# Weight parts at eight offsets in larger buffers, and backward columns in every other tile of the second up product

## The chip, the cores and the metric

The kernel runs on one core of a Trainium2 chip. The metric is device microseconds of one execution, from the median of several timed runs. Engines are named as in the profile: PE (matmuls; PEld are its weight loads), DVE (elementwise), ACT (activations and casts), POOL and SP (here mostly issuers of DMAs).

## The reference

One layer of a streaming encoder on 512 tokens of width 1024, all in float32: a half-step SwiGLU feed-forward, a mixer of chunked attention and trailing means, a second half-step feed-forward, a final norm.

```python
x = x + 0.5 * swiglu_ffn(rmsnorm(x, ffn1_norm[l]), ffn1_w_gate[l], ffn1_w_up[l], ffn1_w_down[l])
x = x + hybrid_mixer(rmsnorm(x, mix_norm[l]), w_in[l], ...)
x = x + 0.5 * swiglu_ffn(rmsnorm(x, ffn2_norm[l]), ffn2_w_gate[l], ffn2_w_up[l], ffn2_w_down[l])
x = rmsnorm(x, final_norm[l])
...
def swiglu_ffn(x, w_gate, w_up, w_down):      # w_gate, w_up: 1024 x 2816, w_down: 2816 x 1024
    return (jax.nn.silu(x @ w_gate) * (x @ w_up)) @ w_down
```

## The kernel before

**Products of float32 from three matmuls.** Each operand is split into two parts of type float32r, `hi` (a cast by ACT) and `lo` (the rest, by DVE), in `split`, or in `high` and `low` within the up product. `mm3` multiplies hi by hi (L170), hi of the loaded operand by lo of the streamed one (L171), and lo by hi (L172). In a matmul the first argument after the output is the loaded (stationary) operand, 128 columns wide, and the next is streamed, 128, 256 or 512 columns wide; in the profile `mm<-ha,whi` is a matmul into `mm` that streams `ha` and has loaded `whi`.

**Stages.** The first up product (gate and up projections of the first feed-forward, `ffn_up` with `loaded=False`), the first down product (`Down`), the mixer, the second up product (`ffn_up` with `loaded=True`), the second down product. In an up product the weights are loaded and the normalised activations streamed; in a down product the activations (`ah`) are loaded and the weights streamed.

**Up products.** There are 22 tiles of 128 features. The first five are made plainly, with 512 columns a matmul. The other 17 (`for n in range(PLAIN, KF)`) use a Strassen-like scheme: seven products A11, S3, S2, A22, S1, A12, S4 of half size, each made by `product`: four slices times the three matmuls of `mm3`, 12 matmuls with 256 columns (`HT`), 84 a tile. Each `product` writes into half of a PSUM bank, `acc`, `up_lo` or `up_hi`, and ACT or DVE takes it from there. The loop's order on PE, DVE and ACT is written out by hand (`manual_schedule`). The streamed operands `norm.a[...]` are tiles of the h pool (`ha`), of the pool that held x (`xa`) or of the activation pool (`sa`, for S4 alone). The weight parts come in the order 22, 11, 13, 24: from the loaded blocks, or from sums that DVE makes of them.

**Where weight parts lie.** `part_tiles` gives the next pair of buffers of 1024 columns. From `Down.begin` on, `part_rooms` has four places: three times the weight pool and then the activation pool, so every fourth pair lies in the activation pool. In the loop that is the part for 13, which S3 and S1 use. In the down products `Down.weights` takes its parts from the same places, and the plain tiles do through `weights`. The mixer makes its weights in `prepare`, with tiles of its own of the same tags, and does not go through `part_tiles`.

**What sets the order elsewhere.** In the mixer a planner with costs and ranks orders the work; in the down products the framework's scheduler does. The weights come from memory through SP's queue, and POOL's queue makes sums of blocks of the down weights in memory with accumulating DMAs, paced by small `mark` copies.

Of the kernel before, what the change touches and what calls it, by code (L numbers as in the profile page):

```python
# [9 lines left out]
F32R = mybir.dt.float32r  # L10
# [6 lines left out]
P = 128  # L17
# [29 lines left out]
def layer(  # L47
# [44 lines left out]
    def name(what):  # L92
        n_tiles[0] += 1
        return f"{what}_{n_tiles[0]}"

    def temp(dtype=F32):
        return tpool.tile([P, S], dtype, tag="t", name=name("t"))

    def bank(tag="mm", bufs=4):
        return ps.tile([P, S], F32, tag=tag, name=name(tag), bufs=bufs)  # L100

    def abank():
        return bank("a", 4)
# [36 lines left out]

    part_rooms: list = [(wpool, HILO)]
    n_parts = [0]

    def part_tiles():
        pool, bufs = part_rooms[n_parts[0] % len(part_rooms)]
        n_parts[0] += 1
        return (
            pool.tile([P, 1024], F32R, tag=tag, name=name("w" + tag), bufs=bufs)
            for tag in ("hi", "lo")
        )  # L150

    def weights(src, parts=1):
        n = src.shape[-1]
        raw = raw_tile()
        hi, lo = part_tiles()
        for i in range(parts):
            part = slice(i * n // parts, (i + 1) * n // parts)
            nc.sync.dma_start(raw[:, part], src[:, part])
            split(raw[:, part], hi[:, part], lo[:, part])
        return hi, lo  # L160
# [6 lines left out]
    def mm3(acc, a, b, start, stop, further=False):  # L167

        more = dict(skip_group_check=True) if further else {}
        nc.tensor.matmul(acc, a[0], b[0], start=start, stop=False, **more)  # L170
        nc.tensor.matmul(acc, a[0], b[1], start=False, stop=False, **more)  # L171
        nc.tensor.matmul(acc, a[1], b[0], start=False, stop=stop, **more)  # L172

    def cut(pair, lo, n):
        return pair[0][:, lo : lo + n], pair[1][:, lo : lo + n]


    def residual_tiles():
        pairs = [xpool.tile([P, 2 * S], F32, tag=f"x{k}", name=name("x")) for k in range(KD // 2)]
        return [pairs[k // 2][:, k % 2 * S : (k % 2 + 1) * S] for k in range(KD)]  # L180

    x = residual_tiles()
# [208 lines left out]
    def ffn_up(norm, wA, down, loaded):  # L391
# [21 lines left out]
        for kp in range(KD // 2):  # L413
            if not loaded:
                load(2 * kp)
            w = weights(wA[kp], 1 if loaded or kp else 4)
# [7 lines left out]
            for kk in range(2):  # L424
                k = 2 * kp + kk
# [10 lines left out]
        raws, w = {}, {}  # L436

        def fetch(n):

            if n < KF:  # L440
                f = down.order[n]
                raw = raws[n] = down.pool.tile([P, 4 * S], F32, tag="raw", name=name("raw"), bufs=RAW)
                nc.sync.dma_start(raw[:, S : 3 * S], wA[2 * f])
                nc.sync.dma_start(
                    raw.rearrange("p (b c) -> p b c", c=S)[:, 0:4:3],
                    wA[2 * f + 1].rearrange("p (b c) -> p b c", c=S),
                )

        def high(n, what, src):
            hi, lo = (z[:, : src.shape[-1]] for z in part_tiles())  # L450
            nc.scalar.copy(hi, src)  # L451
            w[what] = hi, lo, src

        def low(what):
            hi, lo, src = w[what]
            nc.vector.tensor_tensor(lo, src, hi.bitcast(F32), op=ALU.subtract)  # L456
# [5 lines left out]
        def high11(n):  # L462
            if n < KF:
                high(n, (n, 11), raws[n][:, :S])

        def low11(n):
            if n < KF:
                low((n, 11))

        def sum13(n):  # L470
            if n < KF:
                z = w[n, "odd"] = new_sum()
                raw = raws[n]
                nc.vector.tensor_tensor(z, raw[:, : 2 * S], raw[:, S : 3 * S], op=ALU.add)

        def sum24(n):
            if n < KF:
                z = w[n, "even"] = new_sum()
                raw, odd = raws[n], w[n, "odd"]
                nc.vector.tensor_tensor(z[:, :S], odd[:, :S], raw[:, 2 * S : 3 * S], op=ALU.add)  # L480
                nc.vector.tensor_tensor(z[:, S:], z[:, :S], raw[:, 3 * S :], op=ALU.add)

        def high13(n):
            if n < KF:
                high(n, (n, 13), w[n, "odd"])

        def low13(n):
            if n < KF:
                low((n, 13))

        def high24(n):
            if n < KF:
                high(n, (n, 24), w[n, "even"])

        def low24(n):
            if n < KF:
                low((n, 24))

        for n, f in enumerate(down.order[2 : PLAIN - 1], 2):
            banks = []  # L500
            for j in range(2):
                wj = weights(wA[2 * f + j])
                acc = bank()
# [7 lines left out]
        n, f = PLAIN - 1, down.order[PLAIN - 1]  # L511
# [23 lines left out]
        down.open(range(G - 3, G))  # L535

        def product(acc, part, a, start):
            for k in range(4):
                mm3(
                    acc, cut(part, k * P, P), [z[k] for z in norm.a[a]],  # L540
                    start and k == 0, k == 3, not start,
                )

        def copy(dst, src, scale=1.0):
            nc.scalar.activation(dst, src, AF.Copy, scale=scale)  # L545
# [7 lines left out]
        with tc.manual_schedule(engines={E.PE, E.DVE, E.Activation}):  # L553
            last_silu = last_place = last_sums = nothing
            for n in range(PLAIN, KF):
                f = down.order[n]
                acc, up_lo, up_hi = bank()[:, :HT], bank()[:, :HT], abank()[:, :HT]
                u, z, sg = temp(), temp(), temp()
                w11, w13, w24 = (w[n, i][:2] for i in (11, 13, 24))
                product(acc, w11, A11, True)  # L560
                last_silu()
                last_place()
                high(n, (n, 22), raws[n][:, 2 * S :])
                low((n, 22))
                w22 = w[n, 22][:2]
                copy(u[:, :HT], acc)
                product(up_hi, cut(w13, S, S), S3, True)
                fetch(n + 2)
                high11(n + 1)
                low11(n + 1)  # L570
                last_sums()
                sum13(n + 1)
                copy(z[:, HT:], up_hi, -1.0)
                product(acc, cut(w24, 0, S), S2, False)
                copy(u[:, HT:], acc, -1.0)
                sum24(n + 1)
                product(up_hi, cut(w24, S, S), A22, False)
                nc.vector.tensor_tensor(u[:, HT:], up_hi, u[:, HT:], op=ALU.add)  # L578
                down.make_sums(u[:, HT:])
                product(acc, cut(w13, 0, S), S1, False)  # L580
                copy(z[:, :HT], acc)
                nc.vector.tensor_tensor(z[:, HT:], z[:, :HT], z[:, HT:], op=ALU.add)
                high13(n + 1)
                low13(n + 1)
                high24(n + 1)
                product(up_lo, cut(w22, S, S), A12, True)
                nc.scalar.activation(sg[:, HT:], z[:, HT:], AF.Silu)
                nc.vector.tensor_tensor(u[:, :HT], up_lo, u[:, :HT], op=ALU.add)
                low24(n + 1)
                product(acc, cut(w22, 0, S), S4, False)  # L590

                def last_silu(acc=acc, sg=sg):
                    nc.scalar.activation(sg[:, :HT], acc, AF.Silu, scale=-1.0)

                def last_place(f=f, u=u, sg=sg):
                    down.place(f, u, sg)

                def last_sums(f=f):
                    down.sums(f)

            last_silu()
            last_place()
            last_sums()
# [7 lines left out]
    class Down:  # L611
# [74 lines left out]
        def weights(self, i, g):  # L686

            src = self.rows(i, g)
            n = groups[g][1] * S
            raw = raw_tile()[:, :n]  # L690
            hi, lo = part_tiles()
            if tuple(src.shape[1:]) == (groups[g][1], S):
                load_now(raw.rearrange("p (k c) -> p k c", c=S), src)
                split(raw, hi[:, :n], lo[:, :n])
            else:

                load_now(raw.rearrange("p (d c) -> p d c", d=S // P), src)
                split(
                    raw.rearrange("p (d k c) -> p k d c", d=S // P, c=P),
                    *(z[:, :n].rearrange("p (k d c) -> p k d c", d=S // P, c=P) for z in (hi, lo)),  # L700
                )
            return hi, lo
# [636 lines left out]
    with tc.tile_pool(name="act2", bufs=1, reuse_waits="tile") as apool:  # L1339
        down2.begin(apool)  # L1340

        for half in range(2):
            for t in range(NT):
# [5 lines left out]
                z = temp()  # L1349
# [196 lines left out]
```

## Time and profile before

| | us |
|---|---|
| timed runs: median | 885.51 |
| timed runs: lowest, highest of 3 | 883.26, 889.71 |
| profiled execution: span | 887.8 |
| PE busy in it | 861.2 |
| DVE busy | 710.9 |
| ACT busy | 500.4 |

The span goes from the first to the last instruction of the one profiled execution; the profile gives no other time for that execution. The granted clock averages 0.987 over the span. Busy times of different engines overlap. Matmuls overlap too: one takes 282 ns (256 columns) or some 395 ns (512 columns) from its start to its modelled end, and the next starts long before, so times are read from start to start.

### The profile page before, as it was taken

The page shows a single profiled execution, that of the slowest core. Times are in us where ns is not written, and L with a number is a line of the kernel's source. Part 1 is how long each engine was busy: PE and PEld are TensorE (multiplying, and loading weights), DVE is VectorE, ACT ScalarE, POOL GpSimd, SP SyncE. Part 2 cuts the span into 40 slices and gives each one's busy share as a digit, 9 for nine tenths or more (in the row PEclk, how much of TensorE's full clock was granted, in tenths as well). Part 3 has the DMA queues.
Part 4 walks back from the last instruction along what each step waited for, and adds up shares of the span by engine and source line. Part 5 has one row for each costly group of instructions (what it writes and reads, how often), then busy time and mean ns, then how long its engine had stood idle before and what let it go on. Part 6 is the DMA issues. An engine that isn't in the chain of part 4 may idle for free.

```text
span 887.8 us, 14123 instructions
## 1 busy us (share of the span) xinstructions
PE 861.2 (97%) x5296; PEld 764.4 (86%) x5296; DVE 710.9 (80%) x1128; ACT 500.4 (56%) x852; POOL 122.3 (14%) x197
## 2 busy tenths in 40 slices
PE   9999999999799999989999999999999999899995
PEld 7889999999778887867877788889999999788885
DVE  7899889888668768686777476969889888777897
ACT  7455555555556556547757455445555555565572
POOL 0112222122300000120020000102222112300011
PEclk9999999999899999999999999999999999999998
DMA  7258879797996663222120126247868787997522
GB/s 284 69 170 232 248 202 230 201 219 177 286 274 201 203 200 121 106 83 83 72 72 25 48 95 232 95 124 220 240 218 226 202 210 194 271 344 262 212 97 95
DMA packets 71955, 158.49 MB, mean 179 GB/s; under 512 B 6080, under 2 KB 29136, under 8 KB 71504
## 3 DMA queue, kind: packets, MB, share of 16 engines
q1 hardware_dynamic: 49088, 111.45, 35.6%
q0 software_dynamic: 22656, 46.14, 24.3%
q8 instruction: 41, 0.67, 0.3%
q14 instruction: 26, 0.21, 0.1%
q10 hardware_dynamic: 144, 0.01, 0.0%
HBM read 153.38 MB, written 50.34 MB: 229 GB/s over the span
## 4 chain that ended last, share of the span: by engine, by line
PE 54%; DVE 4%; ACT 1%; DMA 1%; issue 1%; POOLq 0%; POOL 0%; ACTq 0%
PE mm L170 13%; PE mm L171 13%; PE mm L172 13%; PE a L170 3%; PE a L172 3%; PE a L171 3%; PE a L1161 1%; DMA raw<-in_wB_dram 1%; PE a L1107 1%; PE a L1149 1%; DVE t L1028 1%; DVE wlo L123 1%; PE a L1346 0%; PE a L1036 0%; ACT prob L1088 0%
## 5 line engine op out<-in xcount | busy, mean ns | idle before, releaser
L122 ACT CAST whi<-raw 128x1024 fp32r<-128x1024 f32 (+2 forms) x107 | 102.7, 968 | 80.5 <-PE mm L171 20.4
L123 DVE TENSOR_TENSOR wlo<-raw,whi 128x1024 fp32r<-128x1024 f32 (+2 forms) x107 | 119.4, 1121 | 33.6 <-ACT whi L122 32.7
L172 PE MATMUL mm<-ha,wlo 128*128 128x256 f32 x408 | 115.3, 283 | 0.0
L170 PE MATMUL mm<-ha,whi 128*128 128x256 f32 x408 | 115.2, 282 | 0.0
L171 PE MATMUL mm<-ha,whi 128*128 128x256 f32 x408 | 115.2, 282 | 0.0
L545 ACT ACTIVATE t<-mm 128x256 f32<-128x256 f32 x102 | 39.2, 384 | 118.1 <-PE mm L172 117.4
L456 DVE TENSOR_TENSOR wlo<-wsum,whi 128x1024 fp32r<-128x1024 f32 x68 | 83.0, 1221 | 14.4 <-ACT whi L451 14.4
L170 PEld LDWEIGHTS mm<-ha,whi 128*128 128x128 f32 x408 | 78.2, 192 | 0.1
L171 PEld LDWEIGHTS mm<-ha,whi 128*128 128x128 f32 x408 | 77.5, 190 | 0.1
L172 PEld LDWEIGHTS mm<-ha,wlo 128*128 128x128 f32 x408 | 77.5, 190 | 0.0
L666 POOL DMA_DIRECT2D wsum<-in_wB_dram x72 | 71.7, 1150 | 36.5 <-DMA wsum<-wsum 28.3
L170 PE MATMUL mm<-hhi,whi 128*128 128x512 f32 x192 | 75.9, 398 | 0.3 <-ACT whi L122 0.3
L171 PE MATMUL mm<-hlo,whi 128*128 128x512 f32 x192 | 75.7, 395 | 0.0
L172 PE MATMUL mm<-hhi,wlo 128*128 128x512 f32 x192 | 74.9, 392 | 0.0
L170 PE MATMUL mm<-whi,ah 128*128 128x512 f32 x176 | 69.7, 396 | 1.3 <-ACT whi L122 1.3
L664 POOL COPY mark<-t 128x1 f32<-128x1 f32 x40 | 13.3, 332 | 416.4 <-DVE t L578 237.5
L451 ACT CAST whi<-wsum 128x1024 fp32r<-128x1024 f32 x68 | 68.0, 1047 | 4.3 <-PE mm L171 4.1
L171 PE MATMUL mm<-wlo,ah 128*128 128x512 f32 x176 | 69.4, 395 | 0.8 <-DVE wlo L123 0.8
L172 PE MATMUL mm<-whi,ah 128*128 128x512 f32 x176 | 69.3, 394 | 0.0
L456 DVE TENSOR_TENSOR wlo<-raw,whi 128x512 fp32r<-128x512 f32 x68 | 62.4, 953 | 0.5 <-ACT whi L451 0.5
L123 DVE TENSOR_TENSOR ah<-acts,ah 128x512 fp32r<-128x512 f32 (+1 forms) x72 | 47.6, 667 | 17.1 <-ACT ah L122 17.1
L451 ACT CAST whi<-raw 128x512 fp32r<-128x512 f32 x68 | 56.2, 826 | 5.9 <-PE mm L171 4.4
(211 smaller groups left out, 2418.5 us busy)
## 6 DMA issues: line engine op xcount, KB each, us to landing
raw<-in_wA_dram SPq DMA_DIRECT2D x87, 512.0 KB, 5.4
wsum<-in_wB_dram POOLq DMA_DIRECT2D x60, 512.0 KB, 7.6
raw<-wsum SPq DMA_DIRECT2D x40, 512.0 KB, 4.3
raw<-in_wB_dram SPq DMA_DIRECT2D x30, 512.0 KB, 4.7
wsum<-wsum POOLq DMA_DIRECT2D x20, 512.0 KB, 4.9
x<-in_xT_dram SPq DMA_DIRECT2D x16, 256.0 KB, 7.4
raw<-in_wQK_dram SPq DMA_DIRECT2D x8, 512.0 KB, 3.6
raw<-in_wO_dram SPq DMA_DIRECT2D x8, 512.0 KB, 3.4
```

Of the source, the lines that this page charges most:

```text
L122: nc.scalar.copy(hi, src)
L123: nc.vector.tensor_tensor(lo, src, hi.bitcast(F32), op=ALU.subtract)
L170: nc.tensor.matmul(acc, a[0], b[0], start=start, stop=False, **more)
L171: nc.tensor.matmul(acc, a[0], b[1], start=False, stop=False, **more)
L172: nc.tensor.matmul(acc, a[1], b[0], start=False, stop=stop, **more)
L451: nc.scalar.copy(hi, src)
L456: nc.vector.tensor_tensor(lo, src, hi.bitcast(F32), op=ALU.subtract)
L545: nc.scalar.activation(dst, src, AF.Copy, scale=scale)
L664: nc.gpsimd.tensor_copy(mark, after[:, 0:1])
L666: nc.gpsimd.dma_start(self.rows(i, g), self.rows(self.terms[i][at], g), **(dict(accum_op=ALU.add) if at else {}),)
L1028: nc.vector.tensor_tensor(q3, q3, rs[:, t, :].unsqueeze(2).to_broadcast([P, 8, HD]), op=ALU.mult)
L1107: nc.tensor.matmul(sc[i][:, :n], qT[pair][0][a][rows, t * P : (t + 1) * P], kT[pair][0][b][rows, :n], start=a + b == 0, stop=a == 1,)
```

## The change

Parts lie in buffers of 1056 columns in place of 1024, 128 bytes more on each partition, and begin `at` columns of 4 bytes into them. `at` goes through 0, 4, ... 28 with the count of parts, that is 0, 16, ... 112 bytes, shifted by one step after each four parts; both parts of a pair have the same `at`. All other tiles keep their places modulo 128 bytes.

In the half-size tiles of the second up product (`loaded`) with even n (6, 8, ... 20, eight of the 17), `product` hands the streamed operand and the output to `mm3` with the columns reversed. Each result column lands where it did before. The names, shapes and order of the instructions on each engine are the same in both programs.

```diff
@@ part_tiles
     n_parts = [0]
+    back = [False]
 
     def part_tiles():
         pool, bufs = part_rooms[n_parts[0] % len(part_rooms)]
+        at = 4 * ((n_parts[0] + n_parts[0] // 4) % 8)
         n_parts[0] += 1
         return (
-            pool.tile([P, 1024], F32R, tag=tag, name=name("w" + tag), bufs=bufs)
+            pool.tile([P, 1024 + 32], F32R, tag=tag, name=name("w" + tag), bufs=bufs)[:, at : at + 1024]
             for tag in ("hi", "lo")
         )
@@ ffn_up
         def product(acc, part, a, start):
+            b = [[x[:, ::-1] if back[0] else x for x in z] for z in norm.a[a]]
             for k in range(4):
                 mm3(
-                    acc, cut(part, k * P, P), [z[k] for z in norm.a[a]],
+                    acc[:, ::-1] if back[0] else acc, cut(part, k * P, P), [z[k] for z in b],
                     start and k == 0, k == 3, not start,
                 )
@@ ffn_up, the loop over half-size tiles
             for n in range(PLAIN, KF):
+                back[0] = loaded and n % 2 == 0
                 f = down.order[n]
```

## The prediction

> **What bounds the kernel now.** I read the page first, for the engine that ends last, then the groups of instructions, then TensorE (PE) in order of time. From the page:
>
> ```profile
> span 887.8 us, 14123 instructions
> PE 861.2 (97%) x5296; PEld 764.4 (86%) x5296; DVE 710.9 (80%) x1128; ACT 500.4 (56%) x852; POOL 122.3 (14%) x197
> PEclk9999999999899999999999999999999999999998
> PE 54%; DVE 4%; ACT 1%; DMA 1%; issue 1%; POOLq 0%; POOL 0%; ACTq 0%
> L171 PE MATMUL mm<-ha,whi 128*128 128x256 f32 x408 | 115.2, 282 | 0.0
> L170 PE MATMUL mm<-hhi,whi 128*128 128x512 f32 x192 | 75.9, 398 | 0.3 <-ACT whi L122 0.3
> L171 PE MATMUL mm<-wlo,ah 128*128 128x512 f32 x176 | 69.4, 395 | 0.8 <-DVE wlo L123 0.8
> L170 PE MATMUL a<-whi,ah 128*128 128x512 f32 x110 | 43.8, 398 | 1.4 <-ACT ah L125 1.3
> L170 PE MATMUL a<-whi,ah 128*128 128x256 f32 x44 | 12.4, 281 | 0.0
> ```
>
> PE is busy 97% of the span at full granted clock, and its groups have next to no idle time ahead of them. What a matmul is worth is therefore its pitch (start to start), not the 282 or 398 ns of one row, which overlap. The two up products are bound by PE throughout, as the windows show (sum, PE, PEld, DVE, ACT, POOL, clock, DMA):
>
> ```profile
> 620.00:640.00 20.00, 20.00 (x171) 20.00 (x170) 17.79 (x26) 11.16 (x21) 4.46 (x7) 1.00 0.84 238
> 700.00:720.00 20.00, 20.00 (x170) 20.00 (x169) 17.80 (x26) 11.20 (x21) 3.74 (x6) 1.00 0.63 189
> ```
>
> Every nanosecond on a matmul there goes into the span; DVE, next, is busy 17.8 of 20 us, so PE could shed about 11% before DVE took over.
>
> **The pitch, product by product.** The order of time on PE, one tile of the second up product: first row of each of its seven products of 12 matmuls, and the next tile's first.
>
> ```profile
> 620.81 0.28 PE L170 MATMUL a<-ha,whi 128*128 128x256 f32 x1
> ...
> 622.25 0.28 PE L170 MATMUL mm<-ha,whi 128*128 128x256 f32 x1
> ...
> 623.67 0.28 PE L170 MATMUL mm<-ha,whi 128*128 128x256 f32 x1
> ...
> 625.11 0.28 PE L170 MATMUL mm<-sa,whi 128*128 128x256 f32 x1
> ...
> 626.52 0.29 PE L170 MATMUL mm<-ha,whi 128*128 128x256 f32 x1
> ...
> 627.97 0.28 PE L170 MATMUL a<-xa,whi 128*128 128x256 f32 x1
> ...
> 629.38 0.28 PE L170 MATMUL mm<-xa,whi 128*128 128x256 f32 x1
> ...
> 630.82 0.28 PE L170 MATMUL a<-ha,whi 128*128 128x256 f32 x1
> ```
>
> The steps are 1.44 (A22), 1.42 (S1), 1.44 (A12), 1.41 (S4), 1.45 (A11), 1.41 (S3), 1.44 (S2): divided by 12, four products run at 120.2 ns a matmul and three (S1, S4, S3) at 117.8; the tile takes 10.01 us, 119.2 ns on average. The three have something in common in the built program's placement of tiles: tiles of the weight, h and x pools start 32 bytes past a multiple of 128, those of the activation pool 96 bytes past. S1 and S3 take their loaded part from the activation pool (every fourth part lies there) and stream from the others; S4 streams `sa` from the activation pool. So the loaded part stands 64 bytes off the streamed tile, modulo 128, in exactly these three, and 0 in the other four. The down product shows the same with 512 columns, the part now being streamed:
>
> ```profile
> 802.24 0.39 PE L170 MATMUL mm<-whi,ah 128*128 128x512 f32 x1
> ...
> 804.96 0.39 PE L170 MATMUL a<-whi,ah 128*128 128x512 f32 x1
> ...
> 807.67 0.40 PE L170 MATMUL mm<-whi,ah 128*128 128x512 f32 x1
> ...
> 810.44 0.40 PE L170 MATMUL mm<-whi,ah 128*128 128x512 f32 x1
> ```
>
> From 802.24 to 804.96 are 12 matmuls at offset 0, 226.7 ns each; from 807.67 to 810.44 another 12 with a part from the activation pool (offset 64), 230.8 ns each. 256 more columns cost 226.7 - 120.2 = 106.5 ns at offset 0, so a matmul is 106.5 ns for 256 columns plus an overhead of 13.7 ns, whatever its length; offset 64 makes the overhead 11.3 (256 columns) or 17.8 (512). That overhead is what the placement can change.
>
> By the Trainium skill (TensorE: Matmul & The Clock Gate, "Step-by-step: what each phase is for") the load and the stream have separate SBUF read ports, and loading steals nothing from the running matmul; by that rule the placement's term would be zero. The trace differs: 120.2 against 117.8 ns for matmuls alike but for the placement.
>
> **The change, part by part.** Both programs have the same rows in the same order on every engine; nothing is added, removed or moved, and no wait or DMA is new. Only addresses and the direction of two access patterns differ.
>
> (a) *The offsets.* Parts start 0, 16, ... 112 bytes in, and with the shift by one every fourth part each place in a tile runs through all eight. The part now stands at each of eight offsets to the other operand about equally often: two the trace has shown (0, 64), six it has not. Shifted are 2856 matmuls of 256 columns in the up products (2 x 17 tiles x 84) and 3 x 44 = 132 in the down products, and 576 + 528 + 330 = 1434 of 512 columns (three times the groups of 192, 176 and 110); the mixer's own weights stay at 0. Value taken for the six: the middle of the two seen, since the overhead has come out on either side of 13.7. For 256 columns (120.2 + 117.8) / 2 = 119.0 against 119.2 now: -0.2 x 2988 = -0.6 us. For 512 columns now three parts in four at 226.7 and one at 230.8, 227.7 on average, then 228.75: +1.05 x 1434 = +1.5 us. Bounds for the six: below, the load must still be done. Transposes of 128 columns, each with its load, give its floor:
>
> ```profile
> 539.87 1.36 PE L1346 MATMUL a<-ident,x 128*128 128x128 f32 x11
> L1036 PE MATMUL a<-ident,t 128*128 128x128 f32 x32 | 5.2, 276 | 1.4 <-DVE t L1028 1.4
> ```
>
> The last of the 11 lasts some 276 ns, so ten steps take 1.08 us: 108 ns, an overhead of 1.5 on a stream of 106.5. Above, the overhead doubled: 27.4. Six eighths of the 3750 forward matmuls are 2812, so the bounds are -12.2 x 2812 = -34 us and +13.7 x 2812 = +39 us; the spread seen, 3 ns either way, is 8 us.
>
> (b) *Buffers and writers.* ACT and DVE write the parts at the new offsets. Rows that show offsets, same shape:
>
> ```profile
> L123 DVE TENSOR_TENSOR wlo<-raw,whi 128x1024 fp32r<-128x1024 f32 x89 | 108.2, 1221 | 31.9 <-ACT whi L122 31.4 <-ACT root L306 0.4
> L456 DVE TENSOR_TENSOR wlo<-wsum,whi 128x1024 fp32r<-128x1024 f32 x68 | 83.0, 1221 | 14.4 <-ACT whi L451 14.4
> L451 ACT CAST whi<-wsum 128x1024 fp32r<-128x1024 f32 x68 | 68.0, 1047 | 4.3 <-PE mm L171 4.1
> L451 ACT CAST whi<-raw 128x1024 fp32r<-128x1024 f32 x34 | 35.3, 1038 | 0.0
> ```
>
> DVE takes 1221 ns whichever pools its operands lie in, ACT 1038 to 1049 ns. I take nothing. The cover is the 2.2 us in 20 that DVE has free in the up products; without it, 5% on DVE's 710.9 us would be up to 36 us, but that 5% has no row for it.
>
> (c) *Backwards.* For n = 6, 8, ... 20 of the second up product, 8 tiles x 84 = 672 matmuls stream 256 columns from the last to the first and write them so. Nothing in this trace runs backwards. Lower bound: the overhead vanishes down to the load, (108 - 119.2) x 672 = -7.5 us. Upper: half the rate, 2 x 106.5 + 13.7 = 226.7 ns, what 512 columns take now: (226.7 - 119.0) x 672 = +72.4 us. Nothing could hide that, PE being without idle time there; ACT and DVE would wait on it. I take no cost: the same elements are read and written next to each other, once each, and both ends meet the same 1024 bytes. That leaves 119.0: -0.2 x 672, already in (a).
>
> By the Trainium skill (SBUF — State Buffer, "Door 1: The DMA port swizzle") SBUF gives full bandwidth as long as successive accesses hit the same 16-byte line at least twice, which a backward run of 4-byte columns does as well as a forward one; the same passage says that any non-contiguous access pattern in PSUM slows matmuls significantly, and leaves open whether backwards is one. By its first half (c) costs nothing, by its second the first rival holds; no row here shows either.
>
> Sum: -0.6 + 1.5 = **+0.9 us**. The profiled execution's 887.8 us is 0.26% over the median of the timed runs, 885.51; the difference carries over, to 886.4.
>
> **The rivals.**
> - *Backward columns run at half rate* (reading or writing loses its pairing of neighbours): +72.4 us, 958.8. For it: the stream takes one column in 106.5 / 256 = 0.42 ns, while loads get 128 columns in 108 ns, 0.84 ns each, so the stream is already twice as fast as the slower path on this engine and may owe that to ascending pairs. Against: no row shows it. It decides from 13 ns more per backward matmul (8.9 us / 672); there slower by 1% begins.
> - *The backward stream queues behind the load.* Placement matters, so load and stream meet somewhere. If loads go from the last column down, they now cross a forward stream quickly; a backward stream, twice as fast, would run up behind them and follow at their pace: 108 ns for the first 128 columns, 53 for the rest, 13.7 on top, 175 ns. (175 - 119) x 672 = +37.6 us: 924. Against: if loads ascend, the forward stream would do so today, and its overhead is 13.7 ns only.
> - *The six offsets avoid the meeting.* Overhead 8 ns in place of 13.5 on 2812 + 504 matmuls: -5.5 x 3316 = -18 us, 868. For it: offset 64 already saves 2.4 ns on 256 columns. Against: it costs 4.1 on 512.
> - *The change does nothing to the operands' meeting* (only the direction between pools, not the offset, matters): 885.5, inside the forecast.
>
> **How the numbers follow.** Forecast, no measurable change: 0.45, 886.4, its own range 878 to 895 (8 us of seen spread). Half rate 0.22; queueing 0.14; a smaller slowdown of 10 to 20 us by bad offsets 0.05; offsets that pay 0.14. Faster by over 1% (about what a measurement of this kernel tells from no change, 8.9 us) is 0.14, within 1% 0.45, slower 0.41. The likeliest single case is no change, though slower is nearly as likely in sum; 8 in 10 needs the range to reach 868 below and past half rate above, 962.
>
> **What would show it.** Right: in the after trace the 84-matmul tiles of the second up product take 9.9 to 10.1 us, even and odd n alike, the first up product the same; pitches of 12 differ from product to product between 117 and 121 ns; DVE's L123 stays at 1221. Half rate: every other tile takes about 19 us, its matmul rows grow beyond 282 ns, the even tiles alone carry it. Queueing: about 14.7 us. Offsets: odd tiles of the first up product shift too. A DVE or ACT row of 1024 elements that is more than 2% longer would make (b) wrong.

## The result, and the profile after

Over 18 runs each the changed kernel took 890.29 us (888.09 to 895.54) and the kernel before 886.98 us (883.26 to 889.71): a ratio of 1.0042 [1.0027, 1.0057], that is 3.7 us slower (2.4 to 5.1). It is inside the forecast's 1% either way, four times the +0.9 us of its sum. The 886.4 us of the forecast stood on the 885.51 us that before took in three runs; in 18 runs it took 886.98. The two profiled executions differ the other way (spans 886.9 and 887.8 us). Most of that is the clock: the trace of before shows it at 0.94 from 476 to 484 us and at 0.91 from 500 to 520 us, where the trace of after shows 1.00, and a mean of 0.987 against 0.991 is, by estimate, some 3 us of span. So times are taken from the timed runs, and the traces are read for pitches.

From the page of the kernel after, the head, the clock, and groups that correspond to those shown of before (`mm3` is now at L172 to L174):

```profile
span 886.9 us, 14124 instructions
PE 860.5 (97%) x5296; PEld 759.4 (86%) x5296; DVE 711.6 (80%) x1128; ACT 501.3 (57%) x852; POOL 121.8 (14%) x197
PEclk9999999999899999999999999999999999999998
L173 PE MATMUL mm<-ha,whi 128*128 128x256 f32 x408 | 114.7, 281 | 0.0
L172 PE MATMUL mm<-hhi,whi 128*128 128x512 f32 x192 | 76.4, 401 | 0.3 <-ACT whi L122 0.3
L172 PE MATMUL mm<-whi,ah 128*128 128x512 f32 x176 | 70.1, 399 | 0.8 <-ACT whi L122 0.8
```

Busy shares and idle times are as before. The group of 256 columns went from 282 to 281 ns a matmul, that of 512 columns in the plain tiles from 398 to 401: small, and of opposite sign. The windows show the same. Each row is a stretch of time and how much each engine was busy in it, with the instructions begun: a larger count on PE is a shorter pitch. The stretches lie in the first up product, the plain tiles of the second, its half-size tiles, and the second down product. Before:

```profile
60.00:210.00 150.00, 150.00 (x1251) 149.53 (x1250) 134.22 (x188) 83.75 (x150) 33.65 (x50) 1.00 0.82 214
545.00:585.00 40.00, 40.00 (x175) 32.51 (x174) 34.31 (x41) 15.46 (x18) 4.47 (x6) 1.00 0.46 153
620.00:740.00 120.00, 120.00 (x1010) 120.00 (x1009) 105.51 (x148) 66.85 (x121) 24.17 (x39) 1.00 0.80 217
780.00:860.00 80.00, 80.00 (x382) 67.01 (x382) 64.45 (x82) 49.15 (x74) 4.17 (x3) 1.00 0.69 243
```

and after:

```profile
60.00:210.00 150.00, 150.00 (x1257) 149.42 (x1256) 134.45 (x189) 84.57 (x152) 34.15 (x50) 1.00 0.83 213
545.00:585.00 40.00, 40.00 (x174) 32.34 (x173) 34.32 (x41) 14.45 (x17) 4.47 (x6) 1.00 0.47 150
620.00:740.00 120.00, 120.00 (x1016) 120.00 (x1015) 106.20 (x149) 67.05 (x120) 24.17 (x39) 1.00 0.82 217
780.00:860.00 80.00, 80.00 (x380) 66.41 (x379) 63.41 (x81) 48.59 (x73) 4.17 (x3) 1.00 0.71 236
```

PE is full in all of them. It gets through more matmuls in the half-size tiles (1257 for 1251, 1016 for 1010) and fewer of 512 columns (174 for 175, 380 for 382). The first went better than before and the second worse. The differences are small here; the mean pitches below show them better.

**Backward tiles.** PE in order of time, the kernel after: the first row of each product of tile n = 8 of the second up product (backward), then the first of n = 9 (forward) and of n = 10:

```profile
626.27 0.28 PE L172 MATMUL mm<-ha,whi 128*128 128x256 f32 x1
...
627.70 0.28 PE L172 MATMUL a<-xa,whi 128*128 128x256 f32 x1
...
629.11 0.28 PE L172 MATMUL mm<-xa,whi 128*128 128x256 f32 x1
...
630.53 0.28 PE L172 MATMUL a<-ha,whi 128*128 128x256 f32 x1
...
631.95 0.28 PE L172 MATMUL mm<-ha,whi 128*128 128x256 f32 x1
...
633.36 0.28 PE L172 MATMUL mm<-ha,whi 128*128 128x256 f32 x1
...
634.78 0.28 PE L172 MATMUL mm<-sa,whi 128*128 128x256 f32 x1
...
636.21 0.28 PE L172 MATMUL mm<-ha,whi 128*128 128x256 f32 x1
...
646.16 0.28 PE L172 MATMUL mm<-ha,whi 128*128 128x256 f32 x1
```

The backward tile took 9.94 us, the forward one 9.95, where before each took 10.01. Its steps of 12 are 1.41 to 1.43 us, 117.5 to 119.2 ns a matmul. Over the whole loop the mean is 118.42 ns a matmul in tiles with even n and 118.40 in the others.

**512 columns.** The second down product, kernel after, with the rows 12 matmuls apart:

```profile
805.07 0.40 PE L172 MATMUL a<-whi,ah 128*128 128x512 f32 x1
...
807.87 0.39 PE L172 MATMUL mm<-whi,ah 128*128 128x512 f32 x1
...
810.63 0.40 PE L172 MATMUL mm<-whi,ah 128*128 128x512 f32 x1
...
813.40 0.40 PE L172 MATMUL mm<-whi,ah 128*128 128x512 f32 x1
```

The steps are 2.80, 2.76 and 2.77 us, that is 233.3, 230.0 and 230.8 ns. The 226.7 ns of before does not come up.

**The account.** Mean pitches of each kind, worked out from the starts in the two traces. A row is left out where the next start comes late, mostly after a wait (over 150 ns for 256 columns, over 300 ns for 512):

| | matmuls | before, ns | after, ns | change, us |
|---|---|---|---|---|
| up products, 256 columns | 2856 | 119.1 | 118.4 | -2.1 |
| plain tiles, 512 | 576 | 228.7 | 232.6 | +2.2 |
| down products, 512 | 858 | 229.0 | 231.4 | +2.0 |
| mixer, 512, with a weight part | 480 | 228.6 | 231.5 | +1.4 |

Before rounding the sum is +3.6 us, against 3.7 measured (2.4 to 5.1). That the two are so close is in part chance: the account leaves waits out and comes from one execution of each kernel. In the mixer about one row in ten is left out so, so its line is the roughest. Its parts begin at 0 as before, but they share the weight pool, whose buffers grew by 128 bytes.

ACT and DVE, by form, kernel after:

```profile
L123 DVE TENSOR_TENSOR wlo<-raw,whi 128x1024 fp32r<-128x1024 f32 x89 | 108.2, 1221 | 31.4 <-ACT whi L122 31.4
L458 DVE TENSOR_TENSOR wlo<-wsum,whi 128x1024 fp32r<-128x1024 f32 x68 | 83.0, 1221 | 13.9 <-ACT whi L453 12.0 <-PE mm L174 1.9
L453 ACT CAST whi<-wsum 128x1024 fp32r<-128x1024 f32 x68 | 68.0, 1047 | 4.3 <-PE mm L173 4.1
```

1221 and 1047 ns, to the nanosecond as before: the writers do not see the offsets.

### The profile page after: what moved, and what is told of

It reads as the page before. It is cut to its first block, busy times and chain, and to the rows that moved or that the text cites. A ratio compares the mean times of both kernels' runs of the same rounds, so it can differ in the third digit from the quotient of the medians.

```text
span 886.9 us, 14124 instructions
## 1 busy us (share of the span) xinstructions
PE 860.5 (97%) x5296; PEld 759.4 (86%) x5296; DVE 711.6 (80%) x1128; ACT 501.3 (57%) x852; POOL 121.8 (14%) x197
## 4 chain that ended last, share of the span: by engine, by line
PE 54%; DVE 4%; ACT 1%; DMA 1%; issue 1%; POOLq 0%; POOL 0%; ACTq 0%
PE mm L172 13%; PE mm L173 13%; PE mm L174 13%; PE a L172 3%; PE a L174 3%; PE a L173 3%; DMA raw<-in_wB_dram 1%; PE a L1165 1%; PE a L1111 1%; PE a L1153 1%; DVE t L1032 1%; DVE wlo L123 1%; PE a L1350 0%; PE a L1040 0%; ACT prob L1092 0%
## 5 line engine op out<-in xcount | busy, mean ns | idle before, releaser
L172 PE MATMUL mm<-ha,whi 128*128 128x256 f32 x408 | 114.6, 281 | 0.0
L174 PE MATMUL mm<-ha,wlo 128*128 128x256 f32 x408 | 114.6, 281 | 0.0
L458 DVE TENSOR_TENSOR wlo<-wsum,whi 128x1024 fp32r<-128x1024 f32 x68 | 83.0, 1221 | 13.9 <-ACT whi L453 12.0
L173 PEld LDWEIGHTS mm<-ha,whi 128*128 128x128 f32 x408 | 76.8, 188 | 0.1
L172 PEld LDWEIGHTS mm<-ha,whi 128*128 128x128 f32 x408 | 76.8, 188 | 0.1
L174 PEld LDWEIGHTS mm<-ha,wlo 128*128 128x128 f32 x408 | 76.8, 188 | 0.0
L172 PE MATMUL mm<-hhi,whi 128*128 128x512 f32 x192 | 76.4, 401 | 0.3 <-ACT whi L122 0.3
L174 PE MATMUL mm<-hhi,wlo 128*128 128x512 f32 x192 | 75.5, 396 | 0.0
L172 PE MATMUL mm<-whi,ah 128*128 128x512 f32 x176 | 70.1, 399 | 0.8 <-ACT whi L122 0.8
L453 ACT CAST whi<-wsum 128x1024 fp32r<-128x1024 f32 x68 | 68.0, 1047 | 4.3 <-PE mm L173 4.1
L174 PE MATMUL mm<-whi,ah 128*128 128x512 f32 x176 | 70.0, 398 | 0.0
```

## The experiments

Two theories stood at the start. In **P** the pitch goes by the start of the loaded tile against the streamed one modulo 128 bytes, as the prediction had it. In **G** the growth of the buffers matters by itself: 1056 columns are 4224 bytes, so neighbouring buffers no longer start at the same place modulo 256. The direction was the third suspect.

### The direction alone

`back_only` keeps the two edits of the direction and takes the old `part_tiles`:

```diff
-        at = 4 * ((n_parts[0] + n_parts[0] // 4) % 8)
-            pool.tile([P, 1024 + 32], ...)[:, at : at + 1024]
+            pool.tile([P, 1024], ...)
```

> The change's second half alone: parts at their old places, even tiles of the second up product backwards. Theory P (placement modulo 128 bytes sets the overhead, direction costs nothing): as before, 887.0 within 1.3 us, tiles of the second up product 10.01 us for even and odd n alike. Rival D (direction has a price that the offsets' gain on 256 columns hid): slower by 2 to 5 us, even tiles 10.1 us or more.

Measured: 888.15 us beside 887.67 before, ratio 1.0006 [0.9990, 1.0022]. PE, tiles n = 8 (backward), 9 and 10:

```profile
625.39 0.28 PE L171 MATMUL mm<-ha,whi 128*128 128x256 f32 x1
...
635.36 0.28 PE L171 MATMUL mm<-ha,whi 128*128 128x256 f32 x1
...
645.36 0.28 PE L171 MATMUL mm<-ha,whi 128*128 128x256 f32 x1
```

9.97 us backward, 10.00 forward: a whole tile costs no more backward.

### The offsets and larger buffers alone

`offsets_only` is the changed kernel with every tile forward:

```diff
-                back[0] = loaded and n % 2 == 0
+                back[0] = False
```

> The change's first half alone: larger buffers and eight offsets, nothing backwards. Theory P: the whole of the change, 890.3 (ratio 1.004), up tiles about 9.95 us, 512-column matmuls of the plain tiles about 232 ns apart. Rival D: 886 to 888.

Measured: 891.63 us, ratio 1.0052 [1.0034, 1.0070]: the whole loss. Mean pitch 118.36 ns in the half-size tiles, 232.5 in the plain tiles, 231.3 in the down products, as after.

### The larger buffers without offsets

`big_only` goes one step further and leaves the start at 0:

```diff
-        at = 4 * ((n_parts[0] + n_parts[0] // 4) % 8)
+        at = 0
```

> Buffers 128 bytes larger, every part at their start. Modulo 128 all starts are as before. Theory P: no change, 887.0 within 1.3 us; plain tiles settle at 226.7 ns a matmul, up tiles 10.01 us. Rival G (the growth acts: starts of the buffers no longer agree modulo 256 and 512, so that load and stream never settle): most of the change's loss, 889 to 892, plain tiles at 230 ns or more.

Measured: 889.42 us, ratio 1.0024 [1.0006, 1.0041]. Modulo 128 every tile stands here as before; 512 columns nevertheless took 232.0 ns in the plain tiles and 231.0 in the down products. P falls: growth alone brings back the loss of the 512 columns. The half-size tiles gained 0.12 us each, about half of it in S3, the second product here (PE, first rows of A11, S3, S2 and A22):

```profile
646.53 0.29 PE L172 MATMUL mm<-ha,whi 128*128 128x256 f32 x1
...
647.95 0.28 PE L172 MATMUL a<-xa,whi 128*128 128x256 f32 x1
...
649.31 0.28 PE L172 MATMUL mm<-xa,whi 128*128 128x256 f32 x1
...
650.74 0.28 PE L172 MATMUL a<-ha,whi 128*128 128x256 f32 x1
```

S3 took 1.36 us (113.3 ns a matmul), the next 1.43. In S3 the parts lie in the activation pool, and modulo 256 `hi` now starts 64 bytes past the streamed tile and `lo` 192. S1 takes parts at the same two places, though, and ran at 116.4 ns. From S3 came **G2**, a sharper G that the next expectations use: the ordered pair of places of `hi` and `lo`, relative to the streamed tile modulo 256, sets the pitch.

### All tiles in agreement

`pad448` is the kernel before with an unused tile of 448 bytes ahead of each activation pool. All loaded and streamed tiles then start alike modulo 512. `pad192` takes 192 bytes: alike modulo 256, not 512.

```diff
+    with tc.tile_pool(name="pad1", bufs=1) as pad1, tc.tile_pool(name="act1", ...) as apool:
+        pad1.tile([P, 112], F32, name="pad1")      # pad192: [P, 48]; the same ahead of act2
```

> Before, with a tile of 448 bytes that nothing uses ahead of the activation pool, so that all tiles of weights, activations, x and h agree modulo 512. Theory P: S1, S3 and S4 go from 117.8 to 120.2 ns (2.2 x 36 x 34 = +2.7 us, up tiles 10.08 us), down products lose the 230.8 ns of every fourth part (4.1 x 858 / 4 = -0.9 us): 888.8. Rival G gives the same up tiles, but all 512-column matmuls settled at 226.7, also those behind a fourth part: -2 us in the down products and -1 in the plain tiles, 886.7 in all. A rival in which placement has no part: up tiles 10.01, 887.0.

> As pad448 with 192 bytes: the activation pool agrees with the others modulo 256, not modulo 512. Theory G2: as pad448, all products at 120.0 ns, tiles 10.08 us, 512 columns at 226.7, 887.0. If 512 is the modulus: S1, S3 and S4 not at 120.0 (up tiles off 10.08), fourth parts in the down products at 229 ns or more, 888 to 889.

Measured: 887.04 us, ratio 0.9994 [0.9979, 1.0009], and 886.88 us, 0.9997 [0.9977, 1.0017]. The windows of `pad448`, plain and half-size tiles of the second up product:

```profile
545.00:585.00 40.00, 40.00 (x178) 33.10 (x177) 34.62 (x43) 15.20 (x18) 5.61 (x6) 1.00 0.47 152
620.00:740.00 120.00, 120.00 (x1003) 120.00 (x1002) 104.67 (x147) 66.60 (x119) 24.15 (x39) 1.00 0.80 214
```

1003 matmuls of 256 columns where before had 1010, and 178 of 512 for 175. All seven products run at 120.0 ns (tiles of 10.08 us), 512 columns at 227.1 to 227.8 by stage: agreement is the worse case for 256 columns (forward) and the better for 512, and the two cancel. `pad192` gives 120.0 ns too, and 227.0 to 227.7, so agreement modulo 256 is enough.

### Backward everywhere, and a control

`back_all` turns all 34 half-size tiles round, at the old places; `temp7` gives the temporary pool 7 buffers for 8, which the next experiment needs for room.

```diff
+                back[0] = True                                            # back_all
-    tpool = ctx.enter_context(tc.tile_pool(name="temp", bufs=8))
+    tpool = ctx.enter_context(tc.tile_pool(name="temp", bufs=7))          # temp7
```

> All 34 half-size tiles of both up products backwards, parts at their old places: 2856 backward matmuls in place of 672. Theory P: no price, tiles 9.97 us as the backward ones of back_only, 34 x -0.04 = -1.4 us, ratio 0.998 to 1.000. Rival D: four times what back_only may hide within its interval (up to 0.2% each), slower by 2 to 7 us.

> Before with seven temporary buffers in place of eight, for the part of apart that this alone makes. All theories: no change, 887 within 1.5 us; a wait for a temporary would show as PE idle time in the half-size tiles.

Measured: `back_all` 887.83 us, 1.0003 [0.9983, 1.0023]; `temp7` 888.52 us, 1.0014 [0.9994, 1.0033]. Neither differs from before. PE in `back_all`, first rows of A11, S3 and S2:

```profile
644.77 0.28 PE L171 MATMUL mm<-ha,whi 128*128 128x256 f32 x1
...
646.20 0.28 PE L171 MATMUL a<-xa,whi 128*128 128x256 f32 x1
...
647.63 0.28 PE L171 MATMUL mm<-xa,whi 128*128 128x256 f32 x1
```

A11 (same place) and S3 (64 bytes off) both take 1.43 us; forward they take 1.44 and 1.41. Within a product the means are 118.6 ns at the same place and 119.9 at 64, forward 120.0 and 117.9: the direction changes which place is the dearer. Four products gain 1.4 ns a matmul and three lose 2.0, so the tile still takes 10.00 us. The direction is free here in sum, not in every product.

### The low pitch on purpose

`apart` builds what S3 had by chance in `big_only` for all seven products: everything in agreement as in `pad448`, and in `high`, for the half-size tiles only, `hi` 64 and `lo` 192 bytes in.

```diff
-            pool.tile([P, 1024], ...)
-            for tag in ("hi", "lo")
+            pool.tile([P, 1024 + 64], ...)[:, at : at + 1024]
+            for tag, at in (("hi", 16 * apart), ("lo", 48 * apart))   # high: part_tiles(True)
+        pad1.tile([P, 112], F32, name="pad1")                         # and pad2; temp bufs=7
```

> All tiles agree modulo 256 as in pad448 (buffers 256 bytes larger, one of the eight temporary buffers given up for the room), and in the half-size tiles alone the hi part starts 64 bytes and the lo part 192 bytes into its buffer. Theory G2 (the places of hi and lo relative to the streamed tile modulo 256 set the overhead; the pair 64 and 192 settles at 113.3 ns, as S3 did with the larger buffers): all seven products at 113.3 ns, tiles 9.52 us in place of 10.01, 34 x 0.49 = -16.7 us; 512 columns settled at 226.7, -2 more: 868 to 871, ratio 0.981. If agreement modulo 256 is not enough for 512 columns: +5, 875. Rival L (113.3 was luck of the order of products): tiles 9.85 to 10.0, 882 to 887. Rival E (DVE or ACT bind before PE): tiles above 9.6 with PE idle in them.

Measured: 865.75 us (863.92 to 871.54), ratio 0.9769 [0.9736, 0.9802]: 2.3% faster than the kernel before, and faster than the changed one. PE, first rows of a tile's first two products and of the next tile, then two windows:

```profile
638.32 0.28 PE L170 MATMUL mm<-ha,whi 128*128 128x256 f32 x1
...
639.68 0.28 PE L170 MATMUL a<-xa,whi 128*128 128x256 f32 x1
...
647.84 0.28 PE L170 MATMUL mm<-ha,whi 128*128 128x256 f32 x1
```

```profile
545.00:585.00 40.00, 40.00 (x178) 33.14 (x177) 33.91 (x44) 14.83 (x18) 5.61 (x6) 1.00 0.48 151
620.00:740.00 120.00, 120.00 (x1062) 120.00 (x1061) 110.88 (x156) 69.29 (x125) 24.01 (x38) 1.00 0.86 225
```

The tile takes 9.52 us, each product 1.36 (113.3 ns), and PE does 1062 matmuls where it did 1010; a few early tiles of each loop, which hold waits, take 9.6 to 10.2. 34 tiles times 0.49 us are 16.7 us, if all ran so; 1434 matmuls of 512 columns, some 1.4 ns shorter, are 2.0 more. That is 18.7 of the 20.5 us gained; the rest was not followed. The 512 columns, at 227.1 to 227.8 ns by stage, also show that growth as such is not the cost: these buffers grew by 256 bytes and agree modulo 256, where those of `big_only` grew by 128 and do not. DVE is now busy 110.9 us of 120, the next bound.

### Which of hi and lo, and history

G2 says that the ordered pair of places (`hi`, `lo`) sets the pitch. `swapped` takes 192 and 64 bytes, `both64` takes 64 for both; the rest is as in `apart`.

```diff
-            for tag, at in (("hi", 16 * apart), ("lo", 48 * apart))
+            for tag, at in (("hi", 48 * apart), ("lo", 16 * apart))   # swapped
+            for tag, at in (("hi", 16 * apart), ("lo", 16 * apart))   # both64
```

> As apart, with hi 192 and lo 64 bytes in. Theory G2 (the ordered pair matters): the few products that stood so in the larger-buffer kernels ran at 123.5 ns on average, so tiles of 10.1 to 10.4 us, 34 x (0.1 to 0.4) = +3 to +14 us on pad192: 890 to 900. Rival S (any 128 bytes between hi and lo spread the loads): 113.3 ns and 9.52 us as apart, 866.

> As apart, with hi and lo both 64 bytes in. Theory G2: all seven products at 117.8 ns as S1, S3 and S4 of the kernel before, tiles 9.90 us, 34 x -0.18 = -6 us on pad192: 880 to 882. Rival B (what apart gained came from elsewhere, the seven temporaries or the buffers' new size): 866.

Measured: `both64` 876.99 us (873.59 to 881.21), ratio 0.9897 [0.9844, 0.9949]. `swapped` ran in 887.96, 876.78, 868.10 and 876.87 us; the ratio of the last three is 0.9848 [0.9788, 0.9909], and the first is the one whose trace was taken (tiles of 9.99 us, 118.9 ns). (The 123.5 ns of the expectation was too high: without rows that wait, S4 in `big_only` stood so at 118.6 ns.) The granted clock of that execution was 0.988 against 0.991 to 0.993, which by estimate makes 4 us and not 11 to 20, so the spread itself is the finding. The trace of `both64` shows it within one execution. A tile of the first up product, then one of the second, with all the places the same:

```profile
161.37 0.28 PE L170 MATMUL mm<-ha,whi 128*128 128x256 f32 x1
...
171.26 0.28 PE L170 MATMUL mm<-ha,whi 128*128 128x256 f32 x1
```

```profile
688.38 0.28 PE L170 MATMUL mm<-ha,whi 128*128 128x256 f32 x1
...
697.90 0.28 PE L170 MATMUL mm<-ha,whi 128*128 128x256 f32 x1
```

9.89 us (117.8 ns) and 9.52 us (113.3 ns). The second up product began at 117.8 ns too, and changed over after one wait of PE, here in the order of time with its cause in brackets:

```profile
606.17 0.28 PE L172 MATMUL mm<-xa,wlo 128*128 128x256 f32 x1
606.66 0.38 PE L170 MATMUL a<-ha,whi 128*128 128x256 f32 x1 [0.21 <-ACT t L545]
606.88 0.28 PE L171 MATMUL a<-ha,whi 128*128 128x256 f32 x1
```

From there on every tile took 9.52 us. The trace of `swapped` holds two pitches as well. The first rows of A11, S3 and S2 in the first half-size tile of its second up product, and the row after:

```profile
595.24 0.28 PE L170 MATMUL mm<-ha,whi 128*128 128x256 f32 x1
...
596.61 0.28 PE L170 MATMUL a<-xa,whi 128*128 128x256 f32 x1
...
597.97 0.38 PE L170 MATMUL mm<-xa,whi 128*128 128x256 f32 x1
598.18 0.28 PE L171 MATMUL mm<-xa,whi 128*128 128x256 f32 x1
```

A11 and S3 took 1.37 and 1.36 us, 113.3 to 113.9 ns a matmul. After one step of 0.21 us at 597.97, for which the trace names no wait, all that followed settled at 118.9 ns; the first up product went the same way.

So G2 is only half right: a placement allows certain settled pitches, and which of them holds depends on what went before. A loop at 117.8 or 118.9 ns is 17 x (9.89 or 9.99 - 9.52), 6.3 or 8.0 us, longer than one at 113.3. That is of the order of the steps between `swapped`'s 888, 877 and 868, and between the two pairs of runs of `both64` (873.59 and 874.15, 879.84 and 881.21). Only one execution of each kernel was traced, so that the other steps are such loops is not shown. That a pause of PE sets the rhythm was seen in these traces and not tried by itself.

## Why the prediction was right, and where its working was not

**The bound** held: PE is full in the two up products and the second down product, and the time followed the pitch: +3.6 us by the account, +3.7 (2.4 to 5.1) by the runs.

**The direction (c)**, taken at nothing between -7.5 and +72 us, was right in sum, and it was the step that mattered most: half rate and queueing (0.36 together) fell with 9.94 us for a backward tile, and with 2856 backward matmuls in `back_all` at 1.0003. Its reason, the same elements read next to each other, does not cover that single products moved by -1.4 and +2.0 ns a matmul in `back_all`; that these cancel over the seven products of a tile was luck. The Trainium skill (SBUF — State Buffer, "Door 1: The DMA port swizzle") was cited on both sides. The means of backward and forward tiles after, 118.42 and 118.40 ns, agree with its rule of the 16-byte line. The slowdown of its sentence on non-contiguous patterns in PSUM was not seen for a reversed row of 256 columns.

**The writers (b)** were right at nothing: 1221 and 1047 ns.

**The offsets (a)** had the right idea and the wrong sizes, and this is the step that failed. For 256 columns it gave -0.6 us and -2.1 came; for 512 columns it gave 228.75 ns, +1.5 us, where 231.4 to 232.6 ns and +4.3 us came, and +1.4 in the mixer, whose parts it had left out since they "stay at 0". Three things were behind it. The places were taken modulo 128, while the growth by 128 bytes changes every buffer modulo 256, and `big_only` shows that this alone costs 512 columns 2 to 3 ns. The six unseen offsets were given the middle of the two seen; in the grown buffers the 512 columns came out on average above the dearer one (230.8), and what the six cost without growth was not tried. And the rows of before were read as two fixed prices per matmul (226.7 and 230.8, 227.7 on average), where the means were 228.7 and 229.0 already. The errors of the 256 and the 512 columns had opposite signs, so the sum came out nearer than its terms, and that was luck. The sign named for the first up product, tiles of 9.9 to 10.1 us, was met with 9.87 to 10.02.

**The rival of offsets that pay** (868 us, for an overhead of 8 ns) did not happen here: the eight offsets average 118.4 ns, 11.9 over the stream's 106.5. Its price was real. `apart` has 113.3 ns and 865.75 us, with a placement that this change does not make in all its products.

**A placement term of zero**, which the prediction drew from the Trainium skill (TensorE: Matmul & The Clock Gate, "Step-by-step: what each phase is for"), did not come about: the same matmuls run at 120.0 ns (`pad448`), 117.8 and 113.3 (both in `both64`) by placement and history. Where load and stream meet, no run shows.

## What to carry to other kernels

Where PE is full, take the pitch start to start product by product and ask of products alike in shape why they differ: here a start 64 or 192 bytes off between the loaded and the streamed operand was worth 2.3% of the kernel, more than the change under study. A buffer's size is part of its neighbours' addresses, so an edit that only "makes room" moves every tile behind it. A reversed column order on the streamed operand and the output cost nothing in sum here (1.0003 in `back_all`); since it moved single products by up to 2 ns a matmul, look at it per product before pricing it elsewhere.

## What was not expected of the hardware

- The pitch of a 256-column float32r matmul with its load depends on where the loaded and the streamed tiles start modulo 256 bytes: 120.0 ns with all alike, 117.8 to 118.9 or 113.3 with parts 64 or 192 bytes off. For 512 columns, alike was the best seen (227.0 to 227.8 ns by stage), and mixed places cost up to 232.6 on average.
- One placement can have more than one pitch: 117.8 and 113.3 ns in `both64`, with a wait of 0.21 us of PE between them, and 113.3 and then 118.9 in `swapped`. With `hi` at 64 and `lo` at 192 bytes, both loops of `apart` came to 113.3, and came back to it after each wait.
- A reversed column order swaps the places: with tiles alike 118.6 ns backward against 120.0 forward, 64 bytes off 119.9 against 117.9.
- What makes 256 the modulus, and what picks the settled pitch, was not tried and stays open.
